# Moving the batched inverses of an RWKV-7 layer between GpSimd, ScalarE and VectorE, and shifting their transfers and the dense evictions

## The chip, the cores and the metric

The kernel runs on one core of a Trainium2 chip. The metric is device time in microseconds (us) of one launch. TensorE is called PE here, VectorE DVE, ScalarE ACT, GpSimd POOL and SyncE SP. Each engine works through its own list of instructions in order and waits at an instruction until its semaphores allow it. SP computes nothing in this stretch: it issues the DMAs, and a DMA that has to wait holds back all DMAs that stand behind it on SP.

## The reference

Two layers are computed for 1104 token rows (16 meta tokens, 1024 prompt rows and 8 x 8 sample rows) of width 1024: a gated DeltaNet layer (layer 0), then an RWKV-7 layer (layer 1), then a final norm. The change lies in layer 1, whose state update is

```
rkvz = einsum('sbtd,sde->sbte', xs[:4], w_rkvz)          # xs = xn + (xprev - xn) * mu
a  = sigmoid(a0 + (xs[5] @ a1) @ a2)
kk = l2norm((k * k_k).reshape(B, T, H, N))
S  = S * d_t + (S @ -kk_t) b_t^T + v_t k_t^T             # b = kk * a, per head of 64
y  = S @ r_t
```

The kernel does not run this recurrence token by token. In chunks of 64 tokens it needs, for each head and chunk, the inverse of a unit triangular 64 x 64 system built from `kk` and `b`. All dense products run as three products of a high and a low part (`whi`, `wlo` of the weights; a high and a low part of the rows), so that float32 accuracy is kept.

## The kernel before, in words

**The stretch.** Layer 1 begins with its k projection and its decay and rate. After that comes the stretch that this case is about, `projections`: the dense products r (m = 0), v (m = 2) and z (m = 3), each over 8 column blocks of 128 features and up to 3 segments of 384, 384 and 336 rows. That makes 67 dense tiles `d`, each of 24 matmuls on PE (`dense_tile`). After each half tile (12 matmuls) the code calls `gap`, which takes the next entry of a list `plan` and emits what stands there on the other engines. Place 27, say, is what is emitted behind the 28th half tile. The places 134 to 179 have no dense tile left in front of them. The order of instructions on each engine is exactly the order of emission; nothing reorders it here.

**What the places hold.**
- Weights: a DMA `wraw` per half of a column block, its cast `whi` on ACT and `wlo` on DVE (L139, L143), one to three places before PE needs it.
- Mixing (`mix_steps`): the rows of v and z are mixed (`mixs`, ACT then DVE, L115, L2338, L2339) and split into high (ACT, L139) and low (DVE, L143) parts. Ten to fifteen of these fall into the few places where one projection ends and the next begins (43 to 50, and 91 to 98), because they overwrite tiles of the old projection. The parts appear as `xa`, `xc`, `xh`, `xl`.
- Evictions: when a tile `d` is done, its `out` is put at the next place: ACT copies it to `ev` (L2507; for z a tanh on ACT and one DVE operation, L1318), and two places later SP stores it (L2508).
- Systems (`system_steps`): 24 items (segment and head pair), one about every three places. An item loads `sldcs`, `slda`, `sldk` (L1562), makes `al`, `kk` and `a` on ACT and DVE, and 24 small matmuls `frss` and `fL`. It stores `ald` (L1606), `kpd` (L1611), `k2d` (L1615) and, two places later, the systems `rltd` (L1619).
- Inverses: the 24 items form batches 0 to 4 (5, 5, 5, 5 and 4 items). When a batch is complete, its diagonal 32 x 32 blocks are loaded as `invA` (L1636), and `system_inverse` inverts up to 120 of them at once, one per partition: 31 steps of a product and a subtraction (`invtmp`, `invT`, L690, L692), two steps to a place, all on POOL. Then ACT writes the transposed result (L1646, "the turn"), SP stores `r_t` and `r_u` to DRAM (L1650, L1651) and loads `TL` (L1657, L1658). There is one `invT` buffer, so a batch's first memset waits until the last `r_t` has left it.
- Merges: for each item, four DMAs load the inverted blocks into `sTT` (L1666, one of four buffers). Four places later (one place for the fifth item, whose buffer was just in use) PE multiplies (`mZ`, `mU`, L129), ACT copies, and SP stores `ttd` (L1697).

Batch 0's inverse starts at place 27, the turn is at 43, `r_t` and `r_u` at 44, `TL` at 46 and the first `sTT` at 47. Batches 1, 2 and 3 follow 20, 40 and 60 places later, and batch 4 at 107, with its turn at 123, `r_t` at 124, `TL` at 126 and `sTT` from 127. Behind the stretch comes the recurrence of layer 1 (the wave), which also runs the last tiles `zz` of the z projection.

Of the kernel before, what the change touches and what calls it, by code (L numbers as in the profile page):

```python
# [88 lines left out]
class Builder:  # L89
# [581 lines left out]
        L.put(ends[2] + 8, store, 3)  # L671
        return out

    def inverse_open(self, nb, pool):

        T = self.t(pool, [128, 1024], "invT", 1)[0:nb]
        self.nc.gpsimd.memset(T, 0.0)
        self.nc.gpsimd.memset(T[:, 0:1024:33], 1.0)
        return T

    def inverse_steps(self, A, nb, pool, T=None, eng=None):

        nc = self.nc
        v = eng or nc.vector
        T = self.inverse_open(nb, pool) if T is None else T
        Tv = T.rearrange("p (i j) -> p i j", j=32)
        for j in range(31):
            n, m = 31 - j, j + 1
            tmp = self.t(pool, [128, 256], "invtmp", 1)[0:nb, 0:n * m].rearrange("p (n m) -> p n m", m=m)
            v.tensor_tensor(tmp, A[:, j, j + 1:32].unsqueeze(2).broadcast_to([nb, n, m]),  # L690
                            Tv[:, j, 0:m].unsqueeze(1).broadcast_to([nb, n, m]), op=ALU.mult)
            v.tensor_tensor(Tv[:, j + 1:32, 0:m], Tv[:, j + 1:32, 0:m], tmp, op=ALU.subtract)  # L692
            yield Tv
# [880 lines left out]
    def system_steps(self, Q, B):  # L1574

        nc, t, col, pool = self.nc, self.t, self.pcol, B.pool
        pc = lambda x: col[x][:, Q.p:Q.p + 1]
        q = Q.n - B.items[0]
        cs, a, k = (Q.ld[x] for x in ("cs", "a", "k"))
        c6 = lambda x: x.rearrange("p (c i) -> p c i", i=64)  # L1580
        kk, iD = t(pool, [128, 384], "skk", 3), cs
        al, sq = t(pool, [128, 384], "sal", 3), t(pool, [128, 384], "sqs", 3)
        self.act(al[:, 1:384], cs[:, 0:383], AF.Exp, scale=-self.DEC)
        nc.vector.memset(c6(al)[:, :, 0:1], 1.0)
        if Q.s == 0:
            nc.vector.memset(al[:, 0:64].rearrange("p (b r) -> p b r", r=8)[:, :, 0:1], 1.0)
        self.act(sq, k, AF.Square, scale=pc("rwkv_k_k"))
        nc.vector.scalar_tensor_tensor(kk, k, pc("rwkv_k_k"), a, op0=ALU.mult, op1=ALU.mult)
        nc.vector.scalar_tensor_tensor(al, k, pc("rwkv_k_k"), al, op0=ALU.mult, op1=ALU.mult)
        self.act(iD, cs, AF.Exp, scale=self.DEC)  # L1590
        nc.vector.tensor_tensor(kk, kk, iD, op=ALU.mult)
        yield
        self.act(a, a, AF.Identity, scale=pc("rwkv_k_a"), bias=self.omka[:, Q.p:Q.p + 1])
        yield
        ssp = self.ps("f", 2, "rss")
        for c in range(6):
            for h in (0, 1):
                b = slice(64 * h, 64 * h + 64)
                self.mm(ssp[b, c:c + 1], sq[b, 64 * c:64 * c + 64], self.ones[b, 0:1])
        gp = self.ps("f", 2, "L")  # L1600
        for c in range(6):
            for h in (0, 1):
                b, d = slice(64 * h, 64 * h + 64), slice(64 * c, 64 * c + 64)
                self.mm(gp[b, d], al[b, d], kk[b, d])
        nc.vector.tensor_tensor(a, a, k, op=ALU.mult)
        nc.sync.dma_start(self.ald[Q.n], al)  # L1606
        yield
        rk = self.rk2[:, 6 * Q.n:6 * Q.n + 6]
        nc.vector.tensor_scalar(rk, ssp[:, 0:6], 1e-6, None, op0=ALU.add)
        nc.vector.reciprocal(rk, rk)  # L1610
        nc.sync.dma_start(self.kpd[Q.n], kk)  # L1611
        nc.vector.tensor_tensor(c6(sq), c6(gp[:, 0:384]), rk.unsqueeze(2).broadcast_to([128, 6, 64]), op=ALU.mult)
        if Q.s == 0:
            nc.gpsimd.tensor_tensor(sq[:, 0:64], sq[:, 0:64], self.m_strs2, op=ALU.mult)
        nc.sync.dma_start(self.k2d[Q.n], a)  # L1615
        yield
        yield
        yield
        nc.sync.dma_start(B.ltd[6 * q:6 * q + 6].rearrange("c q i -> q c i"), c6(sq))  # L1619
# [18 lines left out]
    def system_inverse(self, B):  # L1638

        nc, t, nth, pool = self.nc, self.t, B.nth, B.pool  # L1640
        nb = 4 * nth
        Av = B.A.rearrange("p (i s) -> p i s", s=32)
        inv = self.inverse_steps(Av.rearrange("p i s -> p s i"), nb, pool, eng=nc.gpsimd)
        for Tv in inv:
            yield
        nc.scalar.copy(Av, Tv.rearrange("p i j -> p j i"))  # L1646
        yield
        ud = self.dram([nb, 1024], f"r{B.b}_u")
        t1d = self.dram([nb // 2, 1024], f"r{B.b}_t")
        nc.sync.dma_start(t1d, Tv[0:nb // 2].rearrange("p i j -> p (i j)"))  # L1650
        nc.sync.dma_start(ud, B.A)  # L1651
        yield
        yield
        B.TL = t(pool, [128, 30, 32], "TL", 1)[:, 0:nth]
        tv = t1d.rearrange("(c p) (s i) -> p s c i", p=2, s=32)
        for p in (0, 1):
            nc.sync.dma_start(B.TL[64 * p + 32:64 * p + 64], B.ltd[:, 64 * p + 32:64 * p + 64, 0:32].rearrange("c i s -> i c s"))  # L1657
            nc.sync.dma_start(B.TL[64 * p:64 * p + 32], tv[p])  # L1658
        B.uv = ud.rearrange("(r c p) (s i) -> r p s c i", r=2, p=2, s=32)
# [717 lines left out]
    def projections(self, xa, xb, ip, opened, tiles, whi, wlo, fetch, cast):  # L2377

        nc, t = self.nc, self.t
# [24 lines left out]
        starts, g = [], 0  # L2404
# [6 lines left out]
        for h in range(6, 48):  # L2411
            g = starts[h // 2]
# [37 lines left out]
        at = 0  # L2450
        for B in batches:
            g = g0(B.items[-1]) + 9
            B.TT, B.m = {}, {}
            put(g, lambda B=B: self.system_diag(B))
            inv = self.system_inverse(B)
            g = at = max(at + 4, g + 2)
            for u in range(31):
                put(g + u // 2, lambda inv=inv: next(inv, None), 3)
            at += 16
            steps(at, inv, 4, 3)  # L2460
            g = at + 4
            for q in range(len(B.items)):
                put(g + 2 * q + (3 if q == 4 else 0), lambda B=B, q=q: self.system_diagonals(B, q))

                def begin(B=B, q=q):
                    B.m[q] = self.system_merge(B, q)
                    next(B.m[q])
                put(g + 4 + 2 * q, begin)
                for u in range(1, 7):
                    put(g + 4 + 2 * q + u, lambda B=B, q=q: next(B.m[q], None), 1)  # L2470
# [24 lines left out]
        for ti, s in order:  # L2495
            m, k = tiles[ti]
            dst = {0: self.rd, 2: self.vd, 3: self.zd}[m]
            for c0, n in SEGS[s:s + 1]:
# [3 lines left out]
                def out(p=p, c0=c0, n=n, m=m, k=k, dst=dst):  # L2502
# [3 lines left out]
                    else:  # L2506
                        nc.scalar.copy(f[:, 0:n], p[:, 0:n])  # L2507
                    put(now[0] + 2, lambda: nc.sync.dma_start(dst[k][:, c0:c0 + n], f[:, 0:n]))  # L2508
                put(now[0], out, 0)
        while now[0] < len(plan):  # L2510
            gap()
        return zin
# [127 lines left out]
```

## Time and profile before

| | |
|---|---|
| median of 3 runs | 2213.72 us (2209.57 to 2225.7) |
| the profiled execution | 2212.86 us, of which the span of its instructions is 2211.2 us |
| mean granted TensorE clock | 0.982 |
| PE busy over the span | 2122.8 us (96%) |
| DVE, ACT, POOL busy | 1418.8, 1263.8 and 1236.7 us |
| the 67 dense tiles of `projections` | from 1393.7 to 1765.4 us |
| PE busy in them | 353.59 of 371.70 us |
| mean granted clock in them | 0.96 |

A row of the windows view gives, for a stretch of time, how long each engine was busy in it and in brackets its instructions, then the granted PE clock and the mean busy share of the DMA engines. In the timeline, a row is start, duration, engine, line, operation, out<-in, shape and count, and in brackets how long the engine had been idle before it and what ended that. An overlap of pipelined instructions makes some rows start before the last one ends.

### The profile page before, as it was taken

What the parts mean: (1) busy time and instruction counts of PE and PEld (TensorE: products, weight loads), DVE (VectorE), ACT (ScalarE), POOL (GpSimd) and SP (SyncE); (2) the same over time, 40 slices, a digit from 0 to 9 for tenths busy, and PEclk for the clock granted to TensorE, in tenths of its full rate; (3) what the DMA queues carried; (4) which work ended last, traced back from release to release, by engine and by line L of the source; (5) the groups of instructions that cost most, each with busy time, mean ns of one, the idle gap of its engine ahead of it and who ended that gap; (6) DMA issues with size and microseconds to landing.
All of it is one profiled execution on the core that took longest, in us unless ns stands there. A gap on an engine that the chain in (4) does not pass through costs nothing.

```text
span 2211.2 us, 55305 instructions
## 1 busy us (share of the span) xinstructions
PE 2122.8 (96%) x20382; PEld 1965.0 (89%) x20382; DVE 1418.8 (64%) x3670; ACT 1263.8 (57%) x3651; POOL 1236.7 (56%) x1858
## 2 busy tenths in 40 slices
PE   8899999999999999989999999998989999999997
PEld 7889989898999989978999999998989977888886
DVE  7868585866757585975436752767547347766765
ACT  6536565566655565645433564755546466677663
POOL 3428677685858585625241451238568646666663
PEclk9999999999999999999999999999999999999997
DMA  4324242424243332435244144686885566656532
GB/s 121 85 70 124 73 126 71 118 77 111 80 112 96 102 108 71 134 82 175 89 143 119 65 121 171 199 257 172 238 241 145 155 190 164 179 150 177 160 113 89
DMA packets 495400, 291.61 MB, mean 132 GB/s; under 512 B 222345, under 2 KB 480506, under 8 KB 495130
## 3 DMA queue, kind: packets, MB, share of 16 engines
q1 hardware_dynamic: 495130, 288.08, 46.2%
q8 instruction: 161, 2.64, 0.5%
q14 instruction: 109, 0.89, 0.1%
HBM read 195.66 MB, written 92.30 MB: 130 GB/s over the span
## 4 chain that ended last, share of the span: by engine, by line
PE 70%; DVE 15%; ACT 5%; DMA 3%; POOL 3%; issue 3%; SPq 1%; DVEq 0%; POOLq 0%; ACTq 0%
PE d L129 15%; PE dz L129 7%; PE dv L129 7%; PE rA L129 6%; PE rA L133 5%; PE do L129 4%; PE zo L129 3%; DVE cvy L634 3%; PE dk L129 2%; PE dq L129 2%; PE fG L129 2%; PE dlora L129 1%; DVE invtmp L690 1%; DMA wraw<-in_gdn_w_out 1%; PE zz L129 1%
## 5 line engine op out<-in xcount | busy, mean ns | idle before, releaser
L143 POOL TENSOR_TENSOR wlo<-wraw,whi 128x512 fp32r<-128x512 f32 x190 | 251.4, 1324 | 222.0 <-ACT whi L139 210.0
L692 POOL TENSOR_TENSOR invT<-invT,invtmp 72x31 f32<-72x31 f32 (+36 forms) x341 | 212.0, 622 | 26.7
L634 DVE SCALAR_TENSOR_TENSOR cvy<-raw,cw,cvy 128x408 f32<-128x408 f32 (+2 forms) x288 | 201.4, 699 | 31.3 <-ACT cvy L115 27.2
L690 POOL TENSOR_TENSOR invtmp<-invA,invT 72x31 f32<-72x31 f32 (+36 forms) x341 | 204.3, 599 | 24.5 <-DMA invA<-rltd 4.1
L129 PE MATMUL d<-xc,whi 128*128 128x384 f32 (+1 forms) x640 | 177.0, 342 | 0.0
L139 ACT CAST whi<-wraw 128x512 fp32r<-128x512 f32 x238 | 145.7, 613 | 23.8 <-DMA wraw<-in_rwkv_w_rkvz 8.6
L129 PE MATMUL dv<-xc,whi 128*128 128x384 f32 (+1 forms) x480 | 154.1, 342 | 0.0
L129 PE MATMUL dz<-xc,whi 128*128 128x384 f32 (+1 forms) x480 | 152.1, 340 | 0.0
L115 ACT ACTIVATE w<-rA,nbp 128x128 f32<-128x128 f32 x144 | 45.1, 364 | 152.0 <-PE rA L129 151.8
L129 PEld LDWEIGHTS d<-xc,whi 128*128 128x128 f32 x640 | 118.0, 191 | 2.1 <-ACT ev L1441 0.4
L129 PE MATMUL d<-xc,wlo 128*128 128x384 f32 (+1 forms) x320 | 105.0, 338 | 2.1 <-DVE wlo L143 2.1
L160 POOL TENSOR_TENSOR ors<-ovar,cvals 128x6 f32<-128x6 f32 x24 | 34.1, 1420 | 124.4 <-DVE ovar L1122 124.4
L129 PE MATMUL dz<-xa,whi 128*128 128x384 f32 (+1 forms) x288 | 102.3, 355 | 0.5 <-DVE zg L906 0.5
L129 PE MATMUL dv<-xa,whi 128*128 128x384 f32 (+1 forms) x288 | 102.1, 354 | 0.0
L129 PE MATMUL d<-xa,whi 128*128 128x384 f32 (+1 forms) x336 | 96.3, 339 | 4.8 <-ACT whi L139 4.3
L1938 POOL TENSOR_SCALAR y<-y,mv,grs 128x64 f32<-128x64 f32 x132 | 81.5, 635 | 33.5 <-DVE grs L164 28.1
L959 POOL TENSOR_SCALAR Sb<-Sb,eglb 128x128 f32<-128x128 f32 x128 | 89.2, 709 | 6.4 <-DMA Sb<-in_state_gdn 3.3
L129 PEld LDWEIGHTS dv<-xc,whi 128*128 128x128 f32 x480 | 89.0, 188 | 3.5 <-issue 3.0
L129 PEld LDWEIGHTS dz<-xc,whi 128*128 128x128 f32 x480 | 89.7, 189 | 0.7 <-issue 0.2
L129 PE MATMUL d<-xh,whi 128*128 128x384 f32 (+1 forms) x256 | 82.8, 336 | 0.9 <-ACT xh L139 0.9
L129 PE MATMUL d<-xl,whi 128*128 128x384 f32 (+1 forms) x256 | 82.9, 337 | 0.2 <-DVE xl L143 0.2
L129 PE MATMUL d<-xh,wlo 128*128 128x384 f32 (+1 forms) x256 | 82.5, 335 | 0.0
(544 smaller groups left out, 7213.4 us busy)
## 6 DMA issues: line engine op xcount, KB each, us to landing
wraw<-in_gdn_w_in SPq DMA_DIRECT2D x96, 256.0 KB
wraw<-in_rwkv_w_rkvz SPq DMA_DIRECT2D x74, 256.0 KB
Sb<-in_state_gdn SPq DMA_DIRECT2D x64, 256.0 KB
wraw<-in_rwkv_w_o SPq DMA_DIRECT2D x48, 256.0 KB
E<-drow SPq DMA_DIRECT2D x24, 384.0 KB
attn<-drow SPq DMA_DIRECT2D x24, 384.0 KB
wraw<-in_gdn_w_out SPq DMA_DIRECT2D x36, 256.0 KB
out_s_gdn<-Sb SPq DMA_DIRECT2D x32, 256.0 KB
```

The lines of the kernel that those rows point to most:

```text
L115: return self.nc.scalar.activation(out, in_, func, bias=bias, scale=scale, **kw)
L129: self.nc.tensor.matmul(out, lhsT, rhs, start=start, stop=stop)
L133: self.nc.tensor.matmul(out, lhsT, rhs, start=start, stop=True, skip_group_check=True)
L139: nc.scalar.copy(hi, x)
L143: e.tensor_tensor(lo, x, hi.bitcast(F32), op=ALU.subtract)
L160: self.nc.gpsimd.tensor_tensor(y, x, half.broadcast_to(sh), op=ALU.pow)
L634: nc.vector.scalar_tensor_tensor(ys[s][:, 0:wd(s)], raws[s][:, k:k + wd(s)], cw[k], ys[s][:, 0:wd(s)], op0=ALU.mult, op1=ALU.add)
L690: v.tensor_tensor(tmp, A[:, j, j + 1:32].unsqueeze(2).broadcast_to([nb, n, m]), Tv[:, j, 0:m].unsqueeze(1).broadcast_to([nb, n, m]), op=AL ...
L692: v.tensor_tensor(Tv[:, j + 1:32, 0:m], Tv[:, j + 1:32, 0:m], tmp, op=ALU.subtract)
L959: nc.gpsimd.tensor_scalar(Sb[g][:, u], Sb[g][:, u], self.eglb[:, hv, 4 * g + u:4 * g + u + 1], None, op0=ALU.mult)
L1938: nc.gpsimd.tensor_scalar(y[:, q], y[:, q], mv[:, q, 0:1], P.rs[:, q:q + 1], op0=ALU.subtract, op1=ALU.mult)
```

## The change

It has five parts.
1. The turn goes from ACT to the engine that made the inverse (`eng.tensor_copy`): POOL for batches 0 to 3, DVE for batch 4.
2. Batch 4's inverse runs on DVE, three steps to a place from place 112, instead of on POOL, two to a place from 107. Its turn stays at place 123.
3. For batches 0 to 3, `r_t`, `r_u`, `TL`, `sTT` and the merges come two places later (46, 48 and 49 on for batch 0). Start and turn keep their places. Batch 4's transfers keep theirs.
4. In `system_steps` the stores `ald` and `kpd` stand behind `k2d`, at the place after it: two places later for `ald`, one for `kpd`.
5. The eviction of each dense tile is emitted one place later, and with it its store.

`tag` is an empty string everywhere, so that the tiles stay the same.

```diff
     def system_steps(self, Q, B):
...
         nc.vector.tensor_tensor(a, a, k, op=ALU.mult)
-        nc.sync.dma_start(self.ald[Q.n], al)
         yield
...
         nc.vector.reciprocal(rk, rk)
-        nc.sync.dma_start(self.kpd[Q.n], kk)
...
         nc.sync.dma_start(self.k2d[Q.n], a)
         yield
+        nc.sync.dma_start(self.ald[Q.n], al)
+        nc.sync.dma_start(self.kpd[Q.n], kk)
         yield
...
     def system_inverse(self, B):
...
-        inv = self.inverse_steps(Av.rearrange("p i s -> p s i"), nb, pool, eng=nc.gpsimd)
+        eng, tag = (nc.vector, "") if B.b == 4 else (nc.gpsimd, "")
+        inv = self.inverse_steps(Av.rearrange("p i s -> p s i"), nb, pool, eng=eng, tag=tag)
         for Tv in inv:
             yield
-        nc.scalar.copy(Av, Tv.rearrange("p i j -> p j i"))
+        eng.tensor_copy(Av, Tv.rearrange("p i j -> p j i"))
...
     def projections(...):
...
             inv = self.system_inverse(B)
-            g = at = max(at + 4, g + 2)
+            at, per = (27, 47, 67, 87, 112)[B.b], 3 if B.b == 4 else 2
             for u in range(31):
-                put(g + u // 2, lambda inv=inv: next(inv, None), 3)
-            at += 16
-            steps(at, inv, 4, 3)
-            g = at + 4
+                put(at + u // per, lambda inv=inv: next(inv, None), 3)
+            put(at + 31 // per + 1, lambda inv=inv: next(inv, None), 3)
+            at = (46, 66, 86, 106, 124)[B.b]
+            steps(at, inv, 3, 3)
+            g = at + 3
...
-                put(now[0], out, 0)
+                put(now[0] + 1, out, 0)
```

On ACT, at the turn of batch 0 (place 43), where v's mixing begins (`mixs` and its high part `xa`; `ev` is the eviction of a dense tile), there stands before:

```order
L139 CAST whi_19955<-wraw_19794 128x512
L115 ACTIVATE mixs_19959<-xb_2581_14082,omu_516 128x64
L115 ACTIVATE mixs_19959<-xb_2581_14082,omu_516 128x320
L115 ACTIVATE mixs_19964<-xb_2582_14083,omu_516 128x64
L115 ACTIVATE mixs_19964<-xb_2582_14083,omu_516 128x320
L1646 COPY invA_19268<-invT_19333 120x1024
L2507 COPY ev_19989<-d_19894 128x384
L139 CAST xa_100<-mixs_19959 128x384
L139 CAST xa_100<-mixs_19964 128x384
```

And in the same place on ACT now:

```order
L139 CAST whi_19953<-wraw_19791 128x512
L115 ACTIVATE mixs_19957<-xb_2581_14082,omu_516 128x64
L115 ACTIVATE mixs_19957<-xb_2581_14082,omu_516 128x320
L115 ACTIVATE mixs_19962<-xb_2582_14083,omu_516 128x64
L115 ACTIVATE mixs_19962<-xb_2582_14083,omu_516 128x320
L139 CAST xa_100<-mixs_19957 128x384
L139 CAST xa_100<-mixs_19962 128x384
```

Between the mixed rows and their high parts, the turn and the eviction are gone; the eviction follows some instructions later.

On SP, around the transfers of batch 0 (`r_t`, `r_u` and `TL` as above), there stands before:

```order
L1611 DMA kpd<-skk_19851 128x384
L1615 DMA k2d<-slda_19727 128x384
L2508 DMA rd<-ev_19907 128x336
L1650 DMA r_t<-invT_19333 60x1024
L1651 DMA r_u<-invA_19268 120x1024
L2353 DMA wraw_20022<-in_rwkv_w_rkvz 128x4x128
L1619 DMA rltd_18435<-sqs_19853 128x6x64
L2508 DMA rd<-ev_19989 128x384
L1657 DMA TL_20063<-rltd_18433 32x30x32
```

And there on SP now:

```order
L1613 DMA k2d<-slda_19723 128x384
L2510 DMA rd<-ev_19882 128x384
L1615 DMA ald<-sal_19848 128x384
L1616 DMA kpd<-skk_19847 128x384
L2354 DMA wraw_20015<-in_rwkv_w_rkvz 128x4x128
L2510 DMA rd<-ev_19951 128x336
L1619 DMA rltd_18435<-sqs_19849 128x6x64
L1651 DMA r_t<-invT_19332 60x1024
L1652 DMA r_u<-invA_19265 120x1024
L2510 DMA rd<-ev_20017 128x384
```

The weights `wraw`, a store and the systems `rltd` now stand ahead of `r_t`, and `ald` and `kpd` behind `k2d`.

On SP, where batch 1's fifth item reloads an `sTT` buffer (places 78 and 79 before), there stands before:

```order
L1697 DMA ttd<-sTT_3242_18439 128x384
L1606 DMA ald<-sal_21426 128x384
L1562 DMA sldcs_21574<-csd 128x384
L1562 DMA slda_21576<-ad 128x384
L1562 DMA sldk_21578<-kd 128x384
L1619 DMA rltd_18437<-sqs_21271 128x6x64
L1611 DMA kpd<-skk_21425 128x384
L1615 DMA k2d<-slda_21249 128x384
L1666 DMA sTT_3242_18439<-r_u 32x6x32 x4
L1636 DMA invA_21607<-rltd_18436 60x32x32 x2
```

And there on SP now:

```order
L1613 DMA k2d<-slda_21231 128x384
L1636 DMA invA_21567<-rltd_18436 60x32x32 x2
L2354 DMA wraw_21588<-in_rwkv_w_rkvz 128x4x128
L1698 DMA ttd<-sTT_3242_18439 128x384
L1615 DMA ald<-sal_21390 128x384
L1616 DMA kpd<-skk_21389 128x384
L2510 DMA vd<-ev_21466 128x384
L1667 DMA sTT_3242_18439<-r_u 32x6x32 x4
```

The load `invA` of batch 3 now stands ahead of the reload, and three DMAs instead of seven lie between the store `ttd` that frees the buffer and the reload.

More of the change, by code (lines that the diff above doesn't have):

```diff
@@ L672, in conv_plan, with inverse_open @@
         return out
-    def inverse_open(self, nb, pool):
-        T = self.t(pool, [128, 1024], "invT", 1)[0:nb]
+    def inverse_open(self, nb, pool, tag=""):
+        T = self.t(pool, [128, 1024], "invT" + tag, 1)[0:nb]
         self.nc.gpsimd.memset(T, 0.0)
@@ L679, in inverse_open, with inverse_steps @@
         return T
-    def inverse_steps(self, A, nb, pool, T=None, eng=None):
+    def inverse_steps(self, A, nb, pool, T=None, eng=None, tag=""):
         nc = self.nc
         v = eng or nc.vector
-        T = self.inverse_open(nb, pool) if T is None else T
+        T = self.inverse_open(nb, pool, tag) if T is None else T
         Tv = T.rearrange("p (i j) -> p i j", j=32)
@@ L688, in inverse_steps @@
             n, m = 31 - j, j + 1
-            tmp = self.t(pool, [128, 256], "invtmp", 1)[0:nb, 0:n * m].rearrange("p (n m) -> p n m", m=m)
+            tmp = self.t(pool, [128, 256], "invtmp" + tag, 1)[0:nb, 0:n * m].rearrange("p (n m) -> p n m", m=m)
             v.tensor_tensor(tmp, A[:, j, j + 1:32].unsqueeze(2).broadcast_to([nb, n, m]),
```

## The prediction

> **What bounds the kernel now.** I read the page first, then the windows of the stretch of the 67 dense tiles, then PE's waits in it.
>
> ```profile
> span 2211.2 us, 55305 instructions
> PE 2122.8 (96%) x20382; PEld 1965.0 (89%) x20382; DVE 1418.8 (64%) x3670; ACT 1263.8 (57%) x3651; POOL 1236.7 (56%) x1858
> ```
>
> ```profile
> core 0: us, PE busy (x) PEld busy (x) DVE busy (x) ACT busy (x) POOL busy (x), PEclk, DMA share, GB/s
> 1393.70:1765.40 371.70, 353.59 (x3762) 334.81 (x3763) 223.77 (x404) 207.50 (x447) 226.80 (x377) 0.96 0.73 205
> 1527.50:1534.30 6.80, 5.82 (x17) 5.42 (x18) 6.80 (x9) 4.82 (x10) 6.17 (x9) 0.50 0.81 205
> 1544.50:1551.30 6.80, 5.51 (x75) 5.27 (x72) 5.72 (x11) 4.79 (x13) 6.25 (x8) 0.50 0.39 107
> 1609.40:1612.80 3.40, 3.40 (x25) 2.96 (x23) 2.81 (x4) 1.62 (x4) 3.16 (x4) 0.50 0.73 195
> 1633.30:1636.70 3.40, 3.40 (x11) 3.40 (x12) 0.00 (x0) 2.02 (x5) 0.01 (x1) 0.50 1.02 228
> 1712.00:1742.00 30.00, 30.00 (x363) 28.30 (x362) 11.96 (x17) 13.98 (x34) 26.70 (x43) 1.00 0.57 167
> ```
>
> PE bounds the kernel, and the change adds and removes no matmul. It can gain only what PE loses, which is idle time and half clock (0.50). Four stretches in half clock lie behind stalls; half of their busy time is lost: 2.9, 2.75, 1.7 and 1.7 us. Who was waited for:
>
> ```profile
> PE mZ L129 <- DMA sTT<-r_u: 5.8, 4, 3.8
> PE d L129 <- ACT whi L139: 4.3, 1, 4.3
> PE d L129 <- DVE wlo L143: 3.1, 2, 2.1
> PE fL L129 <- DVE skk L1591: 1.3, 1, 1.3
> PE d L129 <- ACT xh L139: 0.9, 1, 0.9
> PE d L129 <- DVE xl L143: 0.2, 1, 0.2
> ```
>
> ```profile
> 1607.64 0.24 PE L129 MATMUL mZ<-sTT,TL 32*32 32x32 f32 x2 [1.57 <-DMA sTT<-r_u]
> 1632.19 0.22 PE L129 MATMUL mZ<-sTT,TL 32*32 32x32 f32 x2 [3.84 <-DMA sTT<-r_u]
> 1678.43 0.44 PE L129 MATMUL d<-xc,wlo 128*128 128x384 f32 x1 [2.07 <-DVE wlo L143]
> ```
>
> By place this makes four losses. **v's mixing** (places 49 to 54): 4.3 + 0.9 + 0.2 + 1.3 and 1.0 of `wlo`, 7.7 us idle, and 2.9 + 2.75 at half clock: 13.4. **Place 73**: of the 5.8 us for `sTT`, 1.57 and a small wait of some 0.15, and 1.7 at half clock: 3.4. **Place 79**: the other 4.1 and 1.7: 5.8. **Place 97**: 2.1. Together 24.7 us, the most the change can take from these places.
>
> By the Trainium skill (TensorE: Matmul & The Clock Gate, Part 1: The HAM clock gate) the clock halves after a whole idle window of some 3.4 us that runs free of the kernel; by that rule the wait of 1.57 us would not have halved it, and place 73 would cost 1.7 instead of 3.4. The trace shows 0.50 behind that wait, so the measurement decides.
>
> **Part by part: the turn and the evictions at v's mixing.** ACT and DVE show why PE waits there.
>
> ```profile
> 1517.41 2.08 ACT L1646 COPY invA<-invT 120x1024 f32<-120x1024 f32 x1 [7.87 <-POOL invT L692]
> ```
>
> ```profile
> 1511.47 0.56 DVE L1612 TENSOR_TENSOR sqs<-fL,rk 128x384 f32<-128x384 f32 x1
> 1520.31 1.03 DVE L143 TENSOR_TENSOR xa<-mixs,xa 128x384 fp32r<-128x384 f32 x2 [8.29 <-ACT xa L139]
> 1525.31 0.59 DVE L143 TENSOR_TENSOR xl<-mixs,xh 128x384 fp32r<-128x384 f32 x1
> 1532.09 1.80 DVE L143 TENSOR_TENSOR xl<-mixs,xh 128x384 fp32r<-128x384 f32 x2
> 1545.54 0.99 DVE L1591 TENSOR_TENSOR skk<-skk,sldcs 128x384 f32<-128x384 f32 x1
> ```
>
> ACT stood 7.87 us at the turn for POOL's last steps, copied for 2.08 us, and only then made the high parts `xa` for which DVE waited 8.29 us. From 1520.31 DVE's chain runs almost unbroken to `skk` at 1546.53, the last wait of PE here. With the turn on POOL and the eviction later, ACT goes straight from `mixs` to `xa`, and DVE can start at 1511.47 + 0.56 = 1512.0: 8.3 us sooner. That covers the 7.7 us idle with 0.6 to spare. What eats the spare is POOL. In layer 0 the same inverse runs on DVE beside a `wlo` on POOL:
>
> ```profile
> 922.51 1.31 POOL L143 TENSOR_TENSOR wlo<-wraw,whi 128x512 fp32r<-128x512 f32 x1
> 922.56 1.31 DVE L690 TENSOR_TENSOR invtmp<-invA,invT 72x31 f32<-72x31 f32 x1
> 924.15 0.22 DVE L690 TENSOR_TENSOR invtmp<-invA,invT 72x60 f32<-72x60 f32 x1
> ```
>
> A DVE step that began beside POOL's instruction took as long as that one, 1.31 us, where a larger step alone took 0.22. So the turn, now on POOL amid the mixing, can hold a DVE instruction for its whole length. No row shows it; between the memset of the same 1024 elements and two subtractions of 512 it is 0.96 to 2.65 us:
>
> ```profile
> L677 POOL MEMSET invT<- 120x1024 f32 (+1 forms) x5 | 4.8, 955 | 42.1 <-DMA r_t<-invT 42.1
> L143 POOL TENSOR_TENSOR wlo<-wraw,whi 128x512 fp32r<-128x512 f32 x190 | 251.4, 1324 | 222.0 <-ACT whi L139 210.0
> L690 POOL TENSOR_TENSOR invtmp<-invA,invT 120x31 f32<-120x31 f32 (+25 forms) x155 | 98.0, 632 | 16.1 <-DMA invA<-rltd 4.1
> ```
>
> I take 2 us, near ACT's 2.08 for the same copy. The first low parts also come under POOL's steps: two `xl` took 0.59 alone and 1.80 for two, 0.3 more each. So I let the idle time go, and of the half clock one stretch of 2.9 stay: 7.7 + 2.75 = 10.5. Upper end 13.4; lower end, with both stretches left and eight low parts 0.3 longer, 7.7 − 2.4 = 5.3.
>
> The Trainium skill (GPSIMD Engine Reference, Key points) says that GpSimd shares its SBUF interfaces with VectorE and contends with DVE instructions that read two SBUF inputs, which speaks against a turn on POOL here; the 1.31 us above agrees. By it alone the turn would cost the mixing its own length.
>
> The four dense tiles in flight each have a PSUM buffer of their own (`self.ps("d", 4)`), and a tile evicted 2 to 3 us later still leaves two before its buffer is wanted: cost 0. If that cover were gone, PE would wait the length of one eviction, below.
>
> **Transfers two places later, `ald` and `kpd` later.** At place 73 and 79 SP brought the `sTT` late.
>
> ```profile
> SPq L1606 <- DVE sal L1589: 28.8, 11, 4.7
> ```
>
> ```profile
> 1604.31 1.99 SPq L1666 DMA_DIRECT2D sTT<-r_u  x4
> 1622.16 0.43 SPq L1697 DMA_DIRECT2D ttd<-sTT  x1
> 1629.13 2.01 SPq L1666 DMA_DIRECT2D sTT<-r_u  x4
> 1631.19 1.76 SPq L1636 DMA_DIRECT2D invA<-rltd  x2
> ```
>
> SP stood 28.8 us at `ald` for `sal`, and all DMAs behind it stood too. The `sTT` of place 73 was issued at 1604.31 and used at 1607.64, 1.57 us too late; two of SP's waits on `sal` (28.8 / 11 = 2.6 us each) more than cover that, and they go as the store now stands behind its operand by two places. I take all 3.4 (lower end 0, were another wait to take their place). For place 79 the order is mixed. Between `ttd` and the reload now stand three DMAs instead of seven, but the load of `invA` (1.76 us of issue) is ahead, and the reload still stands one place ahead of its merge and needs 1632.19 − 1629.13 = 3.1 us, while the DMA share there is 1.02. I take a third, 2.0, of 0 to 5.8.
>
> Where a batch's `r_t` leaves later, POOL's next memset starts later (42.1 us of such waits above), which is idle time. From one memset to the next it has to fit 62 steps of about 0.632 = 39 us, the turn of 2 and the transfer; twenty of the 134 places are 371.70 × 20 / 134 = 55 us. Should it run over, SP stands at `r_t` with the weights behind it. I take 0, and at worst the length of the stall at place 97, 2.1.
>
> **Place 97.** ACT stood 1.84 us at an eviction, and DVE 2.14 for the high part behind it:
>
> ```profile
> 1663.89 0.48 ACT L2507 COPY ev<-d 128x384 f32<-128x384 f32 x1 [1.84 <-issue]
> 1665.59 1.87 DVE L143 TENSOR_TENSOR xc<-mixs,xc 128x384 fp32r<-128x384 f32 x2 [2.14 <-ACT xc L139]
> ```
>
> With the eviction a place later the chain starts about 2 us sooner and PE's 2.07 us go: I take 2.0, of 0 to 2.1.
>
> **Batch 4 on DVE.** The steps' cost in layer 0, the clashes included:
>
> ```profile
> L690 DVE TENSOR_TENSOR invtmp<-invA,invT 72x31 f32<-72x31 f32 (+15 forms) x31 | 14.5, 469 | 0.2
> L692 DVE TENSOR_TENSOR invT<-invT,invtmp 72x31 f32<-72x31 f32 (+15 forms) x31 | 12.0, 388 | 1.1
> ```
>
> and the largest form of a step, 256 elements, apart:
>
> ```profile
> L690 DVE TENSOR_TENSOR invtmp<-invA,invT 72x256 f32<-72x256 f32 x1 | 0.4, 411 | 0.0
> ```
>
> That is 26.5 us, and a turn of 1 to 2 us, on top of 11.96 in a window of 30 (places 112 to 122): 39.5 to 40.5. By that DVE falls 10 us behind; `wlo` goes to PE one to three places (2.5 us each) ahead, so PE would stand about 5. But POOL, busy for 26.70 of that window, is now empty there, and the clashes go. Alone, a step takes 0.22 for 60 elements and 0.41 for 256; a mean step has 176, which lies at 0.33: 62 × 0.33 = 20.5. With 11.96 and a turn of 1 that is 33.5, 3.5 us behind, which the places ahead cover. I take 0, of −5 to 0.
>
> **The sum.** 10.5 + 3.4 + 2.0 + 2.0 + 0 = 17.9 us. The profiled execution took 2212.86 us (its span and 1.7 around it), which is 0.9 under the median of 2213.72; I expect 2212.9 − 17.9 = 2195 profiled, and 2196 as the median.
>
> **The rivals.**
> - *All four go.* The mixing has no clash that matters and SP, freed of 28.8 us, is in time at place 79: −24.7, 2189. For it: each stall is one wait with one cause that moves. Against it: the reload's one place.
> - *DVE becomes the bound.* Mixing keeps both stretches in half clock (5.3) and batch 4's inverse costs 26.5 us as in layer 0, so that PE stands 5: 5.3 + 3.4 + 2 + 2 − 5 = 7.7, 2206. For it: the 1.31-us rows. Against it: POOL's empty window.
> - *The reload is late in every batch.* The fifth item's `sTT` stands a place ahead of its merge in four batches, and only one paid. If the wait for the `ttd` ahead of it is now the same in all, three more pay 5.8: 17.4 against 10.5 + 3.4 + 2.0 = 15.9, +1.5: 2215, slower. It decides once SP issues the reload under 3.1 us before PE comes to it. Against it: SP's shorter queue.
> - *The gain is given back.* PE gets to the end of the stretch sooner and stands in the recurrence behind it for what was in time before: about 2213. Against it: batch 4's transfers hang on places that move with PE.
>
> **How the numbers follow.** Forecast 0.42, all four go 0.27, DVE bound 0.19, reload 0.06, given back 0.06. The range reaches from 2187 (all gone and some noise) to 2210, beyond the DVE case. About 1% (22 us) is what a measurement of this kernel can tell from no change. Faster by more needs a gain over 22: all of the second case and a little of the first, 0.28. Slower by more than 1%, several mishaps beyond the third rival, 0.05. The rest, 0.67, is within 1%.
>
> **What would show it.** ACT has no wait on `invT`; DVE's idle time of 8.29 us before the first `xa` is gone and its chain ends by 1539; POOL has a copy `invA<-invT` of 1 to 2.6 us. PE's waits lose `whi` 4.3 and `sTT` at place 73; of the four stretches at 0.50 one or two are left. SP's wait on `sal` is gone. DVE is busy for 30 us or so in places 112 to 122, with steps of 0.2 to 0.45 us and no wait of PE on `wlo`. I am wrong if PE waits at places 113 to 124 for `wlo` or `d`, if the DVE steps there keep 1.3 us, or if new waits on `sTT` stand at the fifth items.

## The result: 0.53% faster, 12 us where 18 were forecast

The changed kernel takes 2205.9 us (median of 12 runs, 2200.1 to 2211.39), the kernel before 2217.01 us (12 runs of the same comparison): ratio 0.9947, with a 95% interval of 0.993 to 0.9965. That is 7.8 to 15.5 us of gain, 11.7 in the middle. Two further comparisons of the same two kernels, made beside the experiments, gave 0.9939 (0.9915 to 0.9963, 6 runs) and 0.9967 (0.995 to 0.9983, 12 runs). The profiled execution took 2206.36 us, against 2212.86 before.

The page of the changed kernel begins:

```profile
span 2204.6 us, 55262 instructions
PE 2119.5 (96%) x20382; PEld 1962.4 (89%) x20382; DVE 1439.3 (65%) x3733; ACT 1255.0 (57%) x3646; POOL 1209.8 (55%) x1800
```

PE executes the same 20382 matmuls. DVE has 63 instructions and 20 us more, POOL 58 instructions and 27 us less: batch 4's inverse has moved. PE's waits, in the changed kernel from 1385 to 1800 us:

```profile
PE mZ L129 <- DMA sTT<-r_u: 7.7, 5, 4.7
...
PE fL L129 <- DVE skk L1591: 1.5, 1, 1.5
PE d L129 <- DVE wlo L143: 1.4, 2, 0.9
...
PE d L129 <- ACT xh L139: 0.5, 1, 0.5
```

`whi` (4.3 before) is gone, the waits for `wlo` have fallen from 3.1 to 1.4, and those for `sTT` have **grown** from 5.8 to 7.7. Where they stand, in the timeline of PE:

```profile
1534.02 0.42 PE L129 MATMUL d<-xh,whi 128*128 128x336 f32 x1 [0.48 <-ACT xh L139]
...
1537.58 1.08 PE L129 MATMUL fL<-skk,sal 64*64 64x64 f32 x24 [1.47 <-DVE skk L1591]
1597.91 0.24 PE L129 MATMUL mZ<-sTT,TL 32*32 32x32 f32 x2 [1.51 <-DMA sTT<-r_u]
1629.97 0.28 PE L129 MATMUL mZ<-sTT,TL 32*32 32x32 f32 x2 [4.72 <-DMA sTT<-r_u]
...
1669.69 0.44 PE L129 MATMUL d<-xc,wlo 128*128 128x384 f32 x1 [0.88 <-DVE wlo L143]
...
1734.65 0.44 PE L129 MATMUL d<-xc,wlo 128*128 128x384 f32 x1 [0.48 <-DVE wlo L143]
```

The first two are v's mixing (7.7 us idle before, 2.25 now, with a smaller wait of 0.30). Then comes place 73, but with another merge than before: the merges come two places later, so that the first item of batch 1 stands where the second stood. The second item, now at place 75, has no wait. Then follow the merge of batch 1's fifth item, which stood at place 79 and now stands at 81, place 97 (2.07 before) and a small new wait at place 123. The windows of the changed kernel show the clock at v's mixing and at the fifth item, and DVE in batch 4's inverse:

```profile
1538.20:1541.60 3.40, 3.40 (x42) 3.22 (x38) 2.79 (x8) 2.05 (x5) 3.09 (x5) 0.50 0.59 146
1626.90:1637.10 10.20, 6.57 (x44) 6.40 (x45) 1.16 (x2) 2.31 (x5) 4.69 (x10) 0.50 0.85 268
1706.00:1734.00 28.00, 27.98 (x330) 26.30 (x328) 25.35 (x68) 13.23 (x33) 0.00 (x0) 1.00 0.51 144
```

Behind v's mixing one stretch of 3.4 us at half clock is left of 13.6. At the fifth item's merge there are now 10.2 instead of 3.4 (6.8 in each of two further profiles). In places 112 to 122 DVE is busy for 25.35 of 28 us, POOL for none, and PE for 27.98 at full clock.

**A measure for the parts.** Executions of the changed kernel lay 16 us apart (2197.0 to 2213.4), most of it outside this stretch, as the last section shows. So I compare kernels also by times within one profile that all of them pass: the first `fL` of the 13th item (place 42), of the 15th (place 56), of the 21st (place 74) and of the 24th (place 83), the end of the last dense tile (place 133) and the end of the span. For the kernel before these are 1509.9, 1558.2, 1613.1, 1646.5, 1765.4 and 2211.2 us.

| us in one profile | 42 to 56 (v's mixing) | 56 to 74 | 74 to 83 (fifth item) | 83 to 133 | 42 to 133 | 133 to the end |
|---|---|---|---|---|---|---|
| before | 48.3 | 54.8 | 33.4 | 118.9 | 255.5 | 445.8 |
| changed | 37.4 | 55.0 | 35.9 | 119.7 | 248.1 | 445.7 |
| changed, second profile | 37.5 | 53.1 | 36.0 | 120.9 | 247.5 | 447.2 |
| changed, third profile | 37.4 | 51.6 | 36.0 | 119.6 | 244.6 | 446.0 |
| before + turn on POOL | 38.7 | 57.0 | 33.0 | 119.0 | 247.8 | 449.5 |
| before + evictions later | 48.3 | 54.8 | 30.2 | 118.2 | 251.5 | 449.6 |
| changed, transfers back | 39.2 | 55.5 | 33.1 | 118.5 | 246.3 | 448.5 |
| changed, `ald`, `kpd` back | 38.9 | 55.6 | 36.6 | 121.1 | 252.2 | 446.9 |
| changed, batch 4 on POOL | 37.4 | 52.5 | 36.1 | 118.1 | 244.1 | 449.6 |
| changed, invA of batch 3 later | 38.8 | 53.1 | 33.3 | 122.3 | 247.6 | 445.3 |
| changed, five sTT buffers | 37.2 | 53.4 | 27.3 | 126.7 | 244.6 | 447.2 |
| five buffers, batch 4 on POOL | 37.5 | 54.9 | 28.9 | 121.8 | 243.1 | 450.8 |
| five buffers, batches 1, 2 earlier | 38.9 | 55.7 | 27.3 | 125.8 | 247.6 | 446.4 |
| both | 38.2 | 58.2 | 29.0 | 120.2 | 245.5 | 447.1 |

The columns of the stalls repeat to 0.1 us in the three profiles of the changed kernel; the column 56 to 74 moves by 3.4, with the wait at place 73 (1.7, 1.3 and none, each with the small wait behind it) and its half clock. Differences under some 3 us in the sums are not told apart by one profile.

The columns do not hold quite the same work. Where the merges come two places later, 48 of PE's small matmuls `mZ` and `mU` leave the column 42 to 56 (24 of them take 0.57 us at full clock, so this is some 1.1 us); 24 come into 56 to 74 and 24 into 83 to 133. From 42 to 133 their number is the same in all kernels.

### The profile page after: what moved, and what is told of

Its sections match the earlier page's. It is cut to its first block, busy times and chain, and to the rows that moved or that the text cites. A ratio compares the mean times of both kernels' runs of the same rounds, so it can differ in the third digit from the quotient of the medians.

```text
span 2204.6 us, 55262 instructions
## 1 busy us (share of the span) xinstructions
PE 2119.5 (96%) x20382; PEld 1962.4 (89%) x20382; DVE 1439.3 (65%) x3733; ACT 1255.0 (57%) x3646; POOL 1209.8 (55%) x1800
## 4 chain that ended last, share of the span: by engine, by line
PE 69%; DVE 16%; DMA 5%; ACT 5%; issue 2%; SPq 2%; POOL 1%; DVEq 0%; POOLq 0%; ACTq 0%
PE d L129 15%; PE dz L129 7%; PE dv L129 7%; PE rA L133 6%; PE rA L129 5%; PE do L129 4%; PE zo L129 3%; DVE cvy L634 3%; PE dk L129 2%; PE fG L129 2%; PE dq L129 2%; DVE invtmp L690 1%; DVE invT L692 1%; PE dlora L129 1%; PE zz L129 1%
## 5 line engine op out<-in xcount | busy, mean ns | idle before, releaser
L692 POOL TENSOR_TENSOR invT<-invT,invtmp 72x31 f32<-72x31 f32 (+27 forms) x310 | 194.7, 628 | 24.3
L690 POOL TENSOR_TENSOR invtmp<-invA,invT 72x31 f32<-72x31 f32 (+27 forms) x310 | 185.8, 599 | 21.1 <-DMA invA<-rltd 3.1
L160 POOL TENSOR_TENSOR ors<-ovar,cvals 128x6 f32<-128x6 f32 x24 | 34.1, 1422 | 124.6 <-DVE ovar L1122 124.6
```

The source lines that it names most:

```text
L160: self.nc.gpsimd.tensor_tensor(y, x, half.broadcast_to(sh), op=ALU.pow)
```

## The experiments

### The two parts that touch v's mixing, each alone

The turn alone, on the kernel before:

```diff
-        nc.scalar.copy(Av, Tv.rearrange("p i j -> p j i"))
+        nc.gpsimd.tensor_copy(Av, Tv.rearrange("p i j -> p j i"))
```

> The kernel before with nothing changed but the engine of the turn: POOL copies in all five batches (in batch 4, whose inverse stays on POOL, too). Theory A (the turn is what held ACT at v's mixing): PE's idle time at places 49 to 54 falls from 7.7 to under 3.5 us, one of the two stretches in half clock goes, place 97 keeps its wait of about 2 us for wlo, places 73 and 79 keep theirs; about 8 us faster than before, ratio 0.996. Rival B (the evictions carry the gain): idle time stays over 6 us, ratio 0.999 to 1.

The evictions alone, on the kernel before:

```diff
-                put(now[0], out, 0)
+                put(now[0] + 1, out, 0)
```

> The kernel before with the eviction of each dense tile one place later and nothing else. Theory A: ACT still stands some 8 us at the turn, so v's mixing keeps 6 us or more idle; only place 97 gains 1 to 2 us: 1 to 3 us faster, ratio 0.999. Rival B: ACT reaches the high parts sooner even so, idle time at v's mixing under 3.5 us, ratio 0.996.

Measured: the turn alone 0.9976 (0.9958 to 0.9995), the evictions alone 0.9998 (0.9975 to 1.002). PE's waits from 1500 to 1570 us with the turn alone:

```profile
PE mZ L129 <- DMA sTT<-r_u: 3.6, 4, 1.3
PE d L129 <- DVE wlo L143: 0.9, 1, 0.9
```

and with the evictions alone:

```profile
PE d L129 <- ACT whi L139: 4.1, 1, 4.1
PE fL L129 <- DVE skk L1591: 1.6, 1, 1.6
PE d L129 <- DVE wlo L143: 1.1, 1, 1.1
PE d L129 <- ACT xh L139: 1.0, 1, 1.0
```

The evictions leave v's mixing as it was (48.3 us); the turn alone takes 9.6 us, with the same merges in the column as before. The whole change takes 10.9 us, of which some 1.1 are the merges that left the column, so the turn accounts for all of the rest. Theory A holds, B falls. But the turn alone brings 3.6 us of new waits for `sTT` at batch 0's merges: `r_t` still stands at place 44 in SP's queue, and SP waits there for POOL, with the loads of `sTT` behind it. At place 97 the evictions alone took 0.3 us (2.07 to 1.81), less than the 1 to 2 expected, and with the turn alone the wait is 2.22 us; in the changed kernel it is 0.88, 0.46 and 0.85 us.

That the evictions alone show 30.2 instead of 33.4 us at the fifth item I had not expected; it is one profile, and its comparison of times finds no gain.

### The fifth item's reload

Five buffers instead of four, so that the fifth item of a batch loads three places earlier and waits for nobody's `ttd`:

```diff
-        self.sTT = [t(ip, [128, 6, 64], f"sTT{q}") for q in range(4)]
+        self.sTT = [t(ip, [128, 6, 64], f"sTT{q}") for q in range(5)]
...
-        T = B.TT[q] = self.sTT[B.items[q] % 4]
+        T = B.TT[q] = self.sTT[B.items[q] % 5]
...
-                put(g + 2 * q + (3 if q == 4 else 0), lambda B=B, q=q: self.system_diagonals(B, q))
+                put(g + 2 * q, lambda B=B, q=q: self.system_diagonals(B, q))
```

> The changed kernel with five sTT buffers instead of four: a batch's fifth item loads three places earlier, into a buffer of its own, and no longer waits for the store ttd of the first. Theory C (the stall at place 81, 5.3 us idle and 3 at half clock, is the reload that SP issues late, behind invA, wraw and ttd): the stall goes, 6 to 8 us under the changed kernel, ratio to before 0.991 to 0.992. Rival D (SP or the DMA engines are simply full there, so whatever is loaded comes late): a stall of 3 us or more shows at another item of batch 1, ratio 0.994 to 0.996.

Batch 3's load of `invA` behind the reload:

```diff
-            put(g, lambda B=B: self.system_diag(B))
+            put(g + 4 if B.b == 3 else g, lambda B=B: self.system_diag(B))
```

> The changed kernel with batch 3's loads of invA four places later, so that they stand behind the fifth item's reload of batch 1 as they did before the change. Theory C (the 3.15 us that SP took to issue invA, now ahead of ttd and the reload, are what made this stall longer): the wait for sTT at place 81 falls from 5.3 us to about 2, 3 to 5 us under the changed kernel, ratio 0.993. Rival D (DMA engines full): the wait stays over 4 us, ratio 0.995.

First the queue of SP in the changed kernel, where the reload is issued:

```profile
1618.98 3.15 SPq L1636 DMA_DIRECT2D invA<-rltd  x2
1622.22 1.88 SPq L2354 DMA_DIRECT2D wraw<-in_rwkv_w_rkvz  x1
1624.20 0.45 SPq L1698 DMA_DIRECT2D ttd<-sTT  x1
...
1627.20 2.14 SPq L1667 DMA_DIRECT2D sTT<-r_u  x4
```

Before the change SP issued `ttd` at 1622.16, and PE began to wait at 1628.35, 6.2 us later. Now it issues `ttd` at 1624.20 and PE begins to wait at 1625.25, 1.05 us later: SP spends 3.15 us on `invA` and 1.88 on `wraw` (0.7 of it a wait) first. The reload follows `ttd` 3.0 us later, where it took 7.0 before: the shorter queue between the two gains 4.0 us, and the later `ttd` loses 5.1. SP stands for 0.9 us in these 3.0 until `ttd` has landed, so the reload could not be much closer. With `invA` behind the reload, `ttd` goes out at 1615.79 and PE begins to wait at 1620.26; now SP stands 2.6 us for the landing of `ttd`, and PE's wait falls from 5.28 (4.72 + 0.56) to 3.39 us, between the 2 of theory C and the 4 of rival D. From place 74 to 83 it is 33.3 us, as before the change. With five buffers PE does not wait for this merge at all, and no other item of batch 1 has a wait of 3 us (the first has 1.59). The window of that kernel around the merge:

```profile
1600.00:1640.00 40.00, 40.00 (x542) 37.86 (x541) 17.07 (x31) 17.77 (x42) 27.14 (x41) 1.00 0.91 262
```

PE is busy for 40.00 of 40 us at full clock, while the DMA engines are no less busy (0.91) than in the changed kernel ahead of its stall (0.87 from 1600.0 to 1625.2 us): so it was not that the DMA engines were full (theory D), but the order on SP and the wait for the one buffer (theory C). Place 74 to 83 takes 27.3 instead of 35.9 us.

Yet neither kernel is measured faster than the changed one: 0.9964 (0.9948 to 0.998) with five buffers, where theory C had 0.991 to 0.992, and 0.9951 (0.9932 to 0.9971) with `invA` later, where it had 0.993. From place 83 on, five buffers lose 7.0 us again (126.7 against 119.7), and `invA` later 2.6, all that it had gained. So 7.0 of the 8.6 us are given back.

### Where the 8.6 us go

PE's waits from 1640 to 1752 us with five buffers:

```profile
PE d L129 <- DVE wlo L143: 4.9, 4, 2.2
PE d L129 <- ACT whi L139: 1.9, 2, 1.3
```

Counted from place 42, PE now comes 9.6 us sooner to place 97 (2.21 us for `wlo`, 0.88 in the changed kernel) and 5.1 us sooner to place 123 (2.13 for `wlo`); between them it waits 1.34 us for `whi`, at place 113, which the expectations call place 110. This one goes back to POOL. SP's wait from 1640 to 1765 us, and in the timeline ACT's casts of the two weights behind it; the second is the one that PE waits for at place 113:

```profile
SPq L1651 <- POOL invT L692: 6.2, 1, 6.2
```

```profile
1694.63 0.62 ACT L139 CAST whi<-wraw 128x512 fp32r<-128x512 f32 x1 [7.16 <-DMA wraw<-in_rwkv_w_rkvz]
...
1698.89 0.62 ACT L139 CAST whi<-wraw 128x512 fp32r<-128x512 f32 x1 [1.93 <-DMA wraw<-in_rwkv_w_rkvz]
```

SP stands 6.2 us at batch 3's `r_t`, since POOL has not finished that inverse, and the weights behind it come late. In the changed kernel it stood 2.3 us (3.6 and 3.2 in the other two profiles), and PE did not wait for it. With `invA` later SP stands 6.2 us at the same `r_t` too, and PE 1.54 for `whi` at place 113. Two edits test the places 113 and 123, on the kernel with five buffers. Batch 4 back on POOL:

```diff
-        eng, tag = (nc.vector, "") if B.b == 4 else (nc.gpsimd, "")
+        eng, tag = (nc.vector, "") if B.b == 5 else (nc.gpsimd, "")
...
-            at, per = (27, 47, 67, 87, 112)[B.b], 3 if B.b == 4 else 2
+            at, per = (27, 47, 67, 87, 107)[B.b], 2
```

> The changed kernel with five sTT buffers and batch 4's inverse and turn on POOL from place 107, as before. With five buffers alone the stall at place 81 went, and 7 us came back behind it (places 97, 110 and 123). Theory J (the wait for wlo at place 123 is DVE's inverse standing ahead of that wlo): this wait of 2.13 us goes, the one for whi at place 110 stays, 2 to 3 us less than five buffers alone between the thirteenth item and the end of the last dense tile, that is 242 us; ratio 0.991 to 0.993. Rival K (PE merely comes sooner to whatever stands next): another wait of 2 us in its place, 244 us or more.

The transfers and merges of batches 1 and 2 earlier:

```diff
-            at = (46, 66, 86, 106, 124)[B.b]
+            at = (46, 64, 84, 106, 124)[B.b]
```

> The changed kernel with five sTT buffers and the transfers and merges of batches 1 and 2 two places earlier (as before the change), so that POOL's memset for batch 3 starts two places earlier. Theory L (SP stood 6.2 us at batch 3's r_t for POOL, and the weights behind it came late to place 110): SP's wait at that r_t falls under 2 us and the wait for whi at place 110 goes; 242 to 243 us from the thirteenth item to the last dense tile. Rival K: another wait of 1 us or more takes its place, 244 us or more; batch 1's merges may wait for sTT again at place 71.

And both:

> Both together: five sTT buffers, the transfers of batches 1 and 2 two places earlier, batch 4 on POOL from place 107. If theories J and L hold and add up: 239 to 241 us from the thirteenth item to the last dense tile, ratio to before 0.990 to 0.992, under the changed kernel. Rival K: 244 us or more, the same time as five buffers alone.

Measured: 0.9971 (0.9953 to 0.999), 0.996 (0.9941 to 0.9979) and 0.9966 (0.9949 to 0.9982), beside the changed kernel again:

> The changed kernel again, as the measure for the three beside it. All theories: 247 to 249 us from the thirteenth item to the end of the last dense tile, as in the two profiles of it so far (248.1 and 247.5), waits for sTT of 4 to 6 us at place 81; ratio to before 0.993 to 0.996.

at 0.9967 (0.995 to 0.9983). None of the three reaches its forecast of 0.990 to 0.993. The third profile of the changed kernel took 244.6 us where 247 to 249 were expected: place 73 had no wait.

Theory J holds for its own wait: with batch 4 on POOL the wait at place 123 is gone, and place 83 to 133 takes 121.8 instead of 126.7 us. The wait for `whi` at place 113, which it had left standing, is gone too, and the whole is 243.1 where 242 was forecast. Theory L holds for its own wait: with the earlier transfers SP's wait for POOL at `r_t` is gone, and the one for `whi` at place 113 with it. But the 247.6 us are no gain at all, as rival K had it. New waits of 1.05 and 0.73 us stand between 1650 and 1663 us, and the one for `whi` ahead of place 97 grows from 0.52 to 0.84. In sum PE waits less from place 83 on (5.0 instead of 6.8 us), but it has 10.2 us at half clock there instead of 3.4, which costs up to 3.4 us more; whether another execution would have them, one profile cannot tell. Both together take 120.2 us from place 83 on, the best with five buffers, and 4.8 us more than five buffers alone between places 56 and 74. Their 245.5 us are in the range of rival K. None of these kernels is measured faster than the changed kernel, so I found no version that beats it. With batch 4 on POOL and five buffers, the recurrence starts late: PE's waits from 1750 to 1780 us there are

```profile
PE fVT L126 <- issue: 2.7, 1, 2.7
PE mU L129 <- ACT sTT L115: 2.0, 2, 1.6
```

where the largest of the changed kernel is 0.96.

### The other three parts, each undone

The transfers of batches 0 to 3 back at 44, 64, 84 and 104:

```diff
-            at = (46, 66, 86, 106, 124)[B.b]
+            at = (44, 64, 84, 104, 124)[B.b]
```

> The changed kernel with r_t, r_u, TL, sTT and the merges of batches 0 to 3 two places earlier, where they were before. Theory A (POOL ends its turn about 10 us later than PE reaches place 44, so SP stands at r_t and all DMAs behind it come late): waits for sTT at batch 0's merges as with the turn alone (0.5 to 1.5 us each) or for whi at places 49 to 54, 2 to 5 us slower than the changed kernel. Rival E (the places of the transfers do not matter, SP is late by its own issue anyway): within 1.5 us of it, and r_t waits at SP without a wait of PE behind.

`ald` and `kpd` back at their places:

```diff
         nc.vector.tensor_tensor(a, a, k, op=ALU.mult)
+        nc.sync.dma_start(self.ald[Q.n], al)
         yield
...
         nc.vector.reciprocal(rk, rk)
+        nc.sync.dma_start(self.kpd[Q.n], kk)
...
         nc.sync.dma_start(self.k2d[Q.n], a)
         yield
-        nc.sync.dma_start(self.ald[Q.n], al)
-        nc.sync.dma_start(self.kpd[Q.n], kk)
         yield
```

> The changed kernel with the stores ald and kpd where they were before. Theory F (SP waited for sal where it was early, so the wait cost nothing): SP's wait for sal comes back with 20 us or more, its wait of wraw for wlo falls from 34 towards 17 us, PE's waits for sTT at places 73 and 81 change by under 1.5 us, time within 2 us of the changed kernel. Rival G (as predicted, the waits for sal made the loads sTT late): PE's waits for sTT grow by 3 us or more, 4 us or more slower.

Batch 4 back on POOL (the edit above, on the changed kernel):

> The changed kernel with batch 4's inverse and turn on POOL from place 107, two steps to a place, as before. Theory H (DVE carries batch 4 for nothing): within 1.5 us of the changed kernel; DVE's busy time at places 112 to 122 falls from 25 to about 12 us; PE's wait of 0.48 us for wlo at place 123 goes. Rival I (the inverse on DVE is a cost): 2 to 4 us faster than the changed kernel.

And the changed kernel beside them:

> The changed kernel itself, as the measure for the three kernels beside it. All theories: ratio to before 0.993 to 0.9965 as measured first; PE's waits again for sTT at places 73 and 81, in sum 5 to 8 us. If those two waits vary by more than 3 us between two executions, a single profile of such a wait carries less than it seems to.

Measured: 0.9961 (0.9943 to 0.998), 0.9966 (0.9951 to 0.9982), 0.9971 (0.9953 to 0.9989), and the changed kernel 0.9939 (0.9915 to 0.9963). The intervals overlap; no part alone is told apart by time.

**Transfers back.** PE's waits from 1500 to 1570 us:

```profile
PE mZ L129 <- DMA sTT<-r_u: 4.0, 3, 2.4
PE fL L129 <- DVE skk L1591: 0.2, 1, 0.2
```

As theory A says, batch 0's merges wait for `sTT` as with the turn alone. But place 42 to 56 costs only 1.8 us more (some 1.1 of it the merges that are back in this column), and place 74 to 83 takes 2.8 us less, 33.1. The two places moved a wait from batch 0 to batch 1 and are worth nothing that these runs can show.

**`ald` and `kpd` back.** SP's wait for `sal` returns with 19.5 us, and its wait of `wraw` for `wlo` falls from 34.1 to 24.3: about half of what had left the one queue place stood at the next. PE's waits for `sTT` are 8.5 us in sum, against 7.7 in the changed kernel, under the 1.5 of theory F; but the stretch takes 252.2 us, 4 more than the slowest of the three changed ones, with 23.9 us at half clock instead of 10 to 17. That lies between F and G, and one profile does not settle the time. At place 73 the profiles say more: SP issues the load for it 8.5 us after PE has passed place 69, where the load is emitted, and PE waits 2.41 us. In the three profiles of the changed kernel these are 7.8, 6.4 and 4.5 us, and 1.7, 1.3 and none.

**Batch 4 on POOL.** The wait for `wlo` at place 123 goes, place 83 to 133 takes 118.1 instead of 119.7 us, and the end behind it 449.6 instead of 445.7 to 447.2. In sum it is 693.7 us from place 42 to the end, against 693.8, 694.7 and 690.6 for the changed kernel: theory H, DVE carries the batch for nothing.

## Why the prediction was right or wrong, step by step

**Right in direction and range, too high by a half.** 2196 us were forecast, 2205.9 measured; a gain of 17.9 forecast, 11.7 measured (7.8 to 15.5). From place 42 to 133 the first profile shows 7.4 of it, the other two 8.0 and 10.9; the kernel before has only one profile, so where the rest lies stays open. The measurement was finer than the 22 us that the prediction allowed for: its interval is 0.35% wide.

**v's mixing: right, by its steps.** 10.5 us of gain were forecast. The column fell by 48.3 − 37.4 = 10.9, some 9.8 without the merges that left it. The parts give 9.4: 5.5 of the 7.7 us idle, and 3.9 of the 5.65 that half clock had cost, as 3.4 of its 13.6 us are left. DVE in the changed kernel at the head and at the end of the chain, and beside POOL's turn:

```profile
1512.79 1.28 DVE L143 TENSOR_TENSOR xa<-mixs,xa 128x384 fp32r<-128x384 f32 x2
...
1521.59 2.83 DVE L143 TENSOR_TENSOR xa<-mixs,xa 128x384 fp32r<-128x384 f32 x2
...
1536.49 0.95 DVE L1591 TENSOR_TENSOR skk<-skk,sldcs 128x384 f32<-128x384 f32 x1
```

```profile
1521.11 2.42 POOL L1647 COPY invA<-invT 120x1024 f32<-120x1024 f32 x1
```

The chain starts at 1512.8 (1512.0 forecast) and ends at 1537.4 (by 1539 forecast). POOL's turn takes 2.42 us, between the bounds of 0.96 and 2.65, and the two `xa` beside it take 2.83 instead of 1.28 us: POOL did hold DVE, for 1.55 us. The first of the two took 2.36 us, and 2.38 and 2.36 in the other two profiles. 2.25 us of the 7.7 are left idle, where I had let all of it go; on the other hand 3.4 us at half clock are left, where I had left 6.8. That the second error makes up for half of the first is luck.

**Place 73: the right cause, too large.** 3.4 us were forecast; the column 56 to 74 gains −0.2, 1.7 and 3.2 in the three profiles. The step that failed is "two of SP's waits on `sal` more than cover that". The load that is used at place 73 is emitted at place 69. Before, SP issued it 8.4 us after PE had passed place 69 (the end of its 840th dense matmul, at 1596.0 us); in the kernels with the evictions alone, the turn alone, and `ald` and `kpd` back it is 8.6, 8.4 and 8.5 us. In the three profiles of the changed kernel it is 7.8, 6.4 and 4.5 us, and in three more kernels that keep the later stores (batch 4 on POOL, `invA` later, five buffers) 5.4, 6.2 and 5.9. So the later stores did make SP less late there, by 0.6 to 3.9 us, not by the 5.2 of two such waits. PE needs only some 10 us from place 69 to 73, and where PE waited for it, the load took 3.3 to 4.2 us from its issue to its use. The load in the first profile of the changed kernel:

```profile
1594.55 1.95 SPq L1667 DMA_DIRECT2D sTT<-r_u  x4
```

It is used at 1597.91. It is also another load than the forecast had in view: that of batch 1's first item, behind the loads `TL`, because the merges came two places later. The second item's load, for which PE waited before, is in time now.

Of SP's 28.8 us at `sal`, only this was left from 1583 to 1640 us in the kernel before, where these loads stand (another wait of 2.0 us lies at 1570.8):

```profile
SPq L1606 <- DVE sal L1589: 2.1, 1, 2.1
```

The rest of SP's lateness there is its own work: in the 56 us from 1576 to 1632 of the changed kernel its waits sum to some 9 us, the longest being 2.8 at a `ttd`, and the rest is one issue behind the other, with hardly a pause. Over the whole stretch much of the wait for `sal` has only changed its place:

```profile
SPq L2354 <- DVE wlo L143: 34.1, 11, 5.7
SPq L1651 <- POOL invT L692: 10.0, 2, 7.7
```

`wraw` waited 16.5 us for `wlo` before, and 34.1 now.

**Place 79, now 81: wrong sign.** 2.0 us of gain were forecast, and place 74 to 83 lost 2.5 (33.4 to 35.9, and 36.0 twice). The step was the price of `invA` ahead of the reload: 1.76 us from its row before, 3.15 where it stands now, and the `wraw` behind it, with 1.88, I had not counted at all though it stands in the quoted order, also ahead of `ttd`. Together they make `ttd` 5.1 us later for PE. What I counted in the change's favour, seven DMAs between `ttd` and the reload that become three, was worth 4.0 us (7.0 to 3.0 from `ttd` to the reload), and more was not to be had, as the reload waits for `ttd` to land. The difference of 1.2 us is what the wait grew by (4.09 to 5.28); the rest of the loss goes with the longer half clock. That is the third rival's mechanism in the one batch that had it before; in the other batches it stayed small, 0.73 us at place 101 (0.49 and 0.18 in the other two profiles, and there 0.66 and 0.70 at place 121).

**Place 97:** 2.0 forecast, 1.2 measured (2.07 to 0.88). The term was too large, and its cause is not shown: with the evictions alone the wait is still 1.81, so the eviction that I named was a small part of it, and with the turn alone it is 2.22.

**Batch 4 on DVE: right.** The steps took 10.5 + 10.4 us (20.5 forecast from the lone steps), the turn 1.12 (1 forecast):

```profile
L692 DVE TENSOR_TENSOR invT<-invT,invtmp 96x31 f32<-96x31 f32 (+15 forms) x31 | 10.5, 339 | 1.1
L690 DVE TENSOR_TENSOR invtmp<-invA,invT 96x31 f32<-96x31 f32 (+15 forms) x31 | 10.4, 337 | 0.8
L1647 DVE COPY invA<-invT 96x1024 f32<-96x1024 f32 x1 | 1.1, 1121 | 0.0
```

It costs PE 0.48 us at place 123 (1.12 and 0.21 in the other two profiles). With five buffers, where PE is 5.1 us earlier there, the same `wlo` costs 2.13, and goes with the inverse.

**POOL's batches.** "Cost 0" was right for the changed kernel, though SP stands 2.3 us at batch 3's `r_t`. The margin is used up: with PE earlier this becomes 6.2 us at SP and 1.34 at PE.

**The signs of being wrong.** Two of those that the prediction named did appear, both small: the wait for `wlo` at place 123, and the new waits for `sTT` at the fifth items of batches 2 and 3. Most of the others came as named: ACT's wait for `invT` and its `whi` wait of 4.3 us are gone. The wait for `sTT` at place 73 was to go, and in two of three profiles it did not.

**The rivals.** *All four go* would have needed both loads of `sTT` in time. Had they been, some would have been given back: where the fifth item's stall was taken away altogether, 7 of 8.6 us were lost again by place 133, so that the sum of stalls in one profile was probably more than the change could take. *The gain is given back* in the recurrence did not come: 445.7 us behind place 133, against 445.8.

## What to carry to other kernels

Read a DMA queue's waits in the few places where PE waits for a load, not summed over the stretch. Compare when PE passed the place at which the load is emitted with when SP issued it: that lateness, against the time that PE needs to the use, says what can be gained. Here 28.8 us of waits taken from one place in the queue made the late load 0.6 to 3.9 us less late, and what was put ahead of a late DMA cost its issue.

Stalls in one profile don't add up to what can be gained: here the next engine stood behind each, with some microseconds of slack. Take one away altogether by an experiment, and see how much comes out at the end.

When the whole varies by more than the change is worth, compare times between two fixed instructions of the same profile, and more than one profile of a kernel. Count the work between the two instructions first: a change that moves work past one of them looks like a gain in one column and a loss in the next.

## What the runs showed of the hardware

**POOL beside DVE.** While POOL wrote a strided copy of 1024 elements (2.42 us), two DVE operations of 384 elements took 2.83 instead of 1.28 us. With POOL idle, DVE's 62 steps took 20.9 us for 96 partitions, though in layer 0, beside POOL's `wlo`, they had taken 26.5 for 72.

**The clock varies most.** In the second profile of the changed kernel PE was busy for 20.5 us without a break, early in layer 0, and ran all of it at half clock (there its 128x384 matmuls start every 0.32 us, at full clock every 0.18):

```profile
149.10:169.60 20.50, 20.50 (x157) 17.83 (x157) 4.35 (x12) 3.56 (x9) 1.27 (x1) 0.50 0.10 34
```

In the first profile the same window ran at full clock:

```profile
149.10:169.60 20.50, 20.50 (x213) 18.59 (x212) 10.04 (x22) 8.76 (x27) 8.87 (x15) 1.00 0.34 95
```

The three profiles of the changed kernel had 24, 38 and 14 us at half clock ahead of the stretch and came to place 42 at 1510.9, 1516.9 and 1504.8 us. That is 12 us between executions of the same program, as much as the change is worth, and as much as half of the time at half clock differs (19 and 7 us). By the Trainium skill (TensorE: Matmul & The Clock Gate, Part 1: The HAM clock gate) the full clock comes back after one busy window of some 3.4 us; the 20.5 us above, with PE busy throughout, do not agree with it.
